# Two DMA queues for x, a new split of the first norm's squares, and fewer idle matmuls at the start

## The chip, the cores and the metric

The kernel runs on one core of a Trainium2 chip. The core has TensorE (PE in the profile) for matrix products, VectorE (DVE) and GpSimd (POOL) for elementwise work, ScalarE (ACT) for functions, and SyncE (SP), which here only issues DMAs. The engines run side by side, each through its own instructions in order, and wait for each other by semaphores. What counts is the device time in microseconds (us). The kernel before took 880.53 us as the median of three runs (880.15 to 881.44).

## What is computed

A two-layer decoder trunk over 1024 positions of width 1024, in float32. Each layer normalises x, scales and shifts it by vectors made from a condition c, mixes it, and adds the gated result to x:

```python
c_act = jax.nn.silu(c)
for layer in range(DEPTH):
    mod = c_act @ ada_w[layer] + ada_b[layer]
    shift, scale, gate = jnp.split(mod, 3, axis=-1)
    h = rmsnorm(x, norm_g[layer]) * (1.0 + scale[:, None, :]) + shift[:, None, :]
    ...  # layer 0: one projection, sliding-window and forgetting attention; layer 1: a recurrent block
    x = x + gate[:, None, :] * y
return rmsnorm(x, final_g)
```

The rmsnorm needs, for each position, the sum of the squares of its 1024 values before anything else can be computed from x. The change concerns that first sum and what stands before it.

## The kernel before

x comes transposed: 128 partitions hold the features, in KT = 8 tiles of 128 features each, and the positions lie along the free axis, in two halves of 512. `xh[0]` and `xh[1]` are the two halves, each of 8 tiles of 128x512 (256 KB each). `col` (128x144) holds every vector that is needed by feature: c, the norm weights, the biases.

The start does this, in this order of program text. GpSimd writes the identity and a tile of ones. SP issues the DMA of `col` (line 149). From c in `col`, ScalarE and VectorE make `cact` = silu(c) (lines 174 to 179); two dummy activations on `tiny2` (lines 180 and 181) have ScalarE load the table that holds Sqrt. From line 415 on, all engines keep the order of the text (`ordered |= ALL`): `load_x(0)` issues the first half of x on SP in five pieces of 2, 2, 2, 1 and 1 tiles; `load_block(c)` issues blocks of ada0 (two rows of 512 KB for the scale and shift of feature tile c, line 395) and of the gate weights (`raws`, `raw_raws`, line 360 on). GpSimd spreads `cact` into `vb8`, and TensorE transposes that into `crow_ps` (line 430), which VectorE then multiplies with ada0's rows (`mod_first`, line 219: one long VectorE instruction for each row).

`warm(n)` (line 423) lets TensorE multiply ones by ones n times; nothing reads the result. In the profile each such matmul, and each transpose or product of float32, stands as two matmul rows. There are `warm(EARLY)` with 12 at the very start, and `warm(WARM)` with 6 at three places: after the transposes of c, after the sums of squares, and after the spread of the norm's factor.

`squares(0)` (line 398) fills eight tiles with squares, `sq[0]` to `sq[7]`, and adds them in pairs: ScalarE squares tiles 0, 2, 4, 6 and 7, VectorE tiles 1, 3 and 5; GpSimd adds 0 and 1, VectorE adds 2 and 3, 4 and 5, 6 and 7. In the profile sq[4], sq[5] are `sq_pth` and sq[6], sq[7] are `sq_ptl`. `norm_sums` then adds over the features on TensorE: each of the four sums gives four matmuls with a two-column right side (eight rows), into `psq_n`. `rstd_of` (line 255) makes the norm's factor from that on VectorE and ScalarE, ending in a copy to `vb_n`; its `spread` has TensorE transpose `vb_n` into `rs_n`. `modulate_in(0, 0, prs)` (line 283) applies factor, scale and shift to tile 0 of x on VectorE (`x`) and ScalarE (`hh`).

Then comes the loop over c = 0 to 7 (line 453): in each step TensorE runs 15 matmuls of 512 columns (`pst`, lines 479 to 483) on tile c of the first half, while the other engines modulate tile c + 1, split its weights into two parts, and load block c + 4. At c = 3 the loop issues further gate weights and `load_x(1)`.

Of the kernel before, what the change touches and what calls it, by code (L numbers as in the profile page):

```python
# [12 lines left out]
F32 = mybir.dt.float32  # L13
F32R = mybir.dt.float32r
AF = mybir.ActivationFunctionType
# [1 line left out]
PSUM = bass.MemoryType.PSUM  # L17

WARM = 6
EARLY = 12  # L20
NS = 5
FIRST = 18
AHEAD = 4
# [1 line left out]
P = 128  # L25
S = 1024
D = 1024
KT = D // P
HALF = 512
# [19 lines left out]
def hybrid_trunk(  # L49
# [23 lines left out]
    ordered = set()  # L73
# [25 lines left out]
    act, dve, gp = Queue("act", nc.scalar), Queue("dve", nc.vector), Queue("gp", nc.gpsimd)  # L99
    pe, sync = Queue("pe", nc.tensor), Queue("sync", nc.sync)  # L100
    ALL = {"act", "dve", "gp", "pe", "sync"}

    def copy(out, in_, scale=1.0):
        act.activation(out, in_, AF.Copy, scale=scale)

    def mul(eng, out, a, b):
        eng.tensor_tensor(out=out, in0=a, in1=b, op=ALU.mult)

    def add(eng, out, a, b):
        eng.tensor_tensor(out=out, in0=a, in1=b, op=ALU.add)  # L110
# [34 lines left out]
    tiny = const.tile([P, 1], F32, name="tiny")  # L145
    gp.memset(tiny, 1e-30)
    tiny2 = const.tile([P, 1], F32, name="tiny2")
    col = const.tile([P, NCOL], F32, name="col")
    sync.dma_start(col, cols)
    nsink = const.tile([P, 8], F32, name="nsink")  # L150
    bfb = const.tile([P, 8], F32, name="bfb")

# [18 lines left out]
        sub(dve, out, l, c)  # L171


    cact = const.tile([P, KT], F32, name="cact")
    ce = const.tile([P, KT], F32, name="ce")
    act.activation(ce, col[:, C_C : C_C + 8], AF.Exp, scale=-1.0)
    dve.tensor_scalar(out=ce, in0=ce, scalar1=1.0, scalar2=None, op0=ALU.add)
    dve.reciprocal(ce, ce)
    mul(dve, cact, ce, col[:, C_C : C_C + 8])
    act.activation(tiny2, cact[:, 0:1], AF.Exp)  # L180
    act.activation(tiny2, tiny2, AF.Sqrt)


    l0 = ctx.enter_context(ExitStack())
    gyp = l0.enter_context(tc.tile_pool(name="gyp", bufs=2, reuse_waits="tile"))
    l0a = ctx.enter_context(ExitStack())
    at = l0a.enter_context(tc.tile_pool(name="at", bufs=2, reuse_waits="tile"))

# [3 lines left out]
    def t4(tag, name, dt=F32, bufs=None):  # L192
        bufs = bufs or BUFS[tag]
        return at.tile([P, 1024], dt, tag=tag, name=name, bufs=bufs)

    xh = []
    for h in range(2):
        t = gyp.tile([P, KT, HALF], F32, tag="gy", name=f"x_{h}")
        xh.append(t)

    mm = pe.matmul

    def tp(out, in_):
        pe.transpose(out, in_, ident)
# [14 lines left out]
    def mod_first(c, part):  # L219

        j = 8 * part + c
        mod_dot(parts[c][part], crow_ps, 0, j, col[:, C_AB0 + j : C_AB0 + j + 1])
        if part:
            g = col[:, C_G0 + c : C_G0 + c + 1]
            act.activation(gsc[:, 0, c : c + 1], mod[:, 0, j : j + 1], AF.Identity, bias=g, scale=g)
# [9 lines left out]
    def norm_sums(sq, w, name, ps=None):  # L235

        psq, steps = sum_steps(sq, w, name, ps)
        for f in steps:
            f()
        return psq  # L240

    def sum_steps(sq, w, name, ps=None):

        psq = (ps or ps_t)(f"psq_{name}")
        sq = sq if isinstance(sq, list) else [sq]

        def step(n, i):
            mm(
                psq[:, 2 * i : 2 * i + 2], sq[n][:, i * P : (i + 1) * P], ones[:, 0:2],
                start=(n == 0 and i == 0), stop=(n + 1 == len(sq) and i + 1 == w // P),  # L250
            )

        return psq, [lambda n=n, i=i: step(n, i) for n in range(len(sq)) for i in range(w // P)]
# [29 lines left out]
    def modulate_in(h, k, prs):  # L283

        x, b = xh[h][:, k], mod[:, 0, k : k + 1]
        dve.scalar_tensor_tensor(out=x, in0=prs, scalar=gsc[:, 0, k : k + 1], in1=x, op0=ALU.mult, op1=ALU.mult)
        act.activation(hh[h][:, k], x, AF.Identity, bias=b)
        act.activation(x, x, AF.Identity, bias=b)
        sub(gp, hlo[h][:, k], x, r32(hh[h][:, k]))
# [28 lines left out]
    def half_of(raw):  # L318
        hi, lo = split_raw(raw[0], [P, 4, P], raw[1])
        return [(hi[:, k], lo[:, k]) for k in range(4)]  # L320
# [20 lines left out]
    gy = [None, None]  # L341
# [25 lines left out]
    def split_start(k):  # L367
        split(raws[k], *(t[:, k % 2] for t in four[k // 2]))
        if k % 4 == 0:
            split(rawb[k], *(t[:, k : k + 4] for t in one))  # L370

    def start_w(i, k):
        return tuple(t[:, k % 2, i] for t in four[k // 2]) if i < 4 else tuple(t[:, k] for t in one)

    def load_x(h):
        for k0, k1 in ((0, 2), (2, 4), (4, 6), (6, 7), (7, 8)):
            sync.dma_start(xh[h][:, k0:k1], xT[:, h, k0:k1])

    hl_ada = {}

    parts = {}
# [1 line left out]
    def load_block(c):  # L383

        if c < 4:
            if c % 2 == 0:
                hl_ada[c // 2] = hl.tile([P, 2, 2, S], F32, tag=f"hl{2 + c // 2}", name=f"ada0_{c}")
            parts[c] = [hl_ada[c // 2][:, c % 2, i] for i in range(2)]
        elif c == 6:
            t = at.tile([P, 2, S], F32, tag="V", name=f"ada0_{c}")  # L390
            parts[c] = [t[:, i] for i in range(2)]
        else:
            parts[c] = [t4("KL" if c == 7 else "P", f"ada0_{c}_{i}") for i in range(2)]
        for i in (1, 0):
            sync.dma_start(parts[c][i], ada0[:, c, i])
        load_start(c)

    def squares(h):

        x = xh[h]  # L400
        t = at.tile([P, 4, HALF], F32, tag="V", name=f"sq_{h}")
        sq = [t[:, i] for i in range(4)]
        sq += [at.tile([P, HALF], F32, tag=t, name=f"sq_{t}_{h}_{i}") for t in ("pth", "ptl") for i in range(2)]
        for k in (0, 2, 4, 6, 7):
            act.activation(sq[k], x[:, k], AF.Square)
        for k in (1, 3):
            mul(dve, sq[k], x[:, k], x[:, k])
        add(dve if h else gp, sq[0], sq[0], sq[1])
        add(dve, sq[2], sq[2], sq[3])
        mul(dve, sq[5], x[:, 5], x[:, 5])  # L410
        for k in (4, 6):
            add(dve, sq[k], sq[k], sq[k + 1])
        return sq[0:KT:2]

    ordered |= ALL
    load_x(0)
    for c in range(4):
        load_block(c)
    vb8 = at.tile([P, KT, P], F32, tag="P", name="vb8", bufs=NP)
# [3 lines left out]
    def warm(n):  # L423
        for _ in range(n):
            mm(pw[:, :P], ones, ones, start=True, stop=True)

    warm(EARLY)
    crow_ps = psX[0].tile([P, S], F32, name="crow_ps")
    for k in range(KT):
        tp(crow_ps[:, k * P : (k + 1) * P], vb8[:, k])  # L430
    warm(WARM)
    sq = squares(0)
    psq = norm_sums(sq, HALF, "n0_0", ps_s)
    mod_first(0, 1)
    warm(WARM)
    spread = rstd_of(psq, HALF, at, ("ptl", "pth"), "n0_0", ps_s)
# [7 lines left out]
    def gate_w(i):  # L444
        return wt[T_GATE + i]

    def gate_raw(i):
        t = t4("P", f"raw_gate_{i}").rearrange("p (k e) -> p k e", k=KT)
        sync.dma_start(t, gate_w(i))
        return [(t[:, 4 * n : 4 * n + 4], f"gate_{i}_{n}") for n in range(2)]  # L450

    ws, graw = [[]], {}
    for c in range(KT):
        if c + 1 < KT:
            split_start(c + 1)
            for i in (1, 0):
                mod_first(c + 1, i)
            modulate_in(0, c + 1, prs)
        if c + 4 < KT:
            load_block(c + 4)  # L460
        if c == 3:
            graw[NS] = []
            for n in range(2):
                t = wp.tile([P, 4, P], F32, tag="wlo", name=f"raw_gate_{n}", bufs=4)
                sync.dma_start(t, gate_w(NS)[:, 4 * n : 4 * n + 4])
                graw[NS].append((t, f"gate_{NS}_{n}"))
            load_x(1)
            for i in range(NS + 1, KT):
                graw[i] = gate_raw(i)
        if c in (5, 6):  # L470
            ws[0] += half_of(graw[NS][c - 5])
        if c == 6:
            for i in range(2):
                copy(crow[:, i * HALF : (i + 1) * HALF], crow_ps[:, i * HALF : (i + 1) * HALF])
            sq = squares(1)
            add(dve, sq[2], sq[2], sq[3])
            add(dve, sq[0], sq[0], sq[1])

        for i in range(NS):
            for n, w in enumerate(start_w(i, c)):  # L480
                mm(sps[i], w, hh[0][:, c], start=(c == 0 and n == 0), stop=False)
        for i in range(NS):
            mm(sps[i], start_w(i, c)[0], hlo[0][:, c], start=False, stop=(c + 1 == KT))
# [23 lines left out]
    psq, steps = sum_steps([sq[2], sq[0]], HALF, "n0_1")  # L507
# [111 lines left out]
    for tb in range(NB):  # L619
        h, o = tb // 4, (tb % 4) * P  # L620
# [54 lines left out]
    for i in range(2):  # L675
        t = t4("P", f"bias_{i}").rearrange("p (h j) -> p h j", h=4)
# [322 lines left out]
    def q_job(ti, name):  # L999
        q = lazy(lambda: qtiles(name))  # L1000
        return q, job(ti, name, lambda h, ps: use_q(q(), name)(h, ps))
# [14 lines left out]
    for p in range(4):  # L1016
        q, jq = q_job(T_AQ + p, f"aq_{p}")
# [19 lines left out]
    k = 0  # L1037
    while ti_ < len(units) or any(x >= k for x in due):
        slot = list(due.pop(k, []))
        if ti_ < len(units) and ti_ in sdone and k > sdone[ti_] + GAP_T:  # L1040
# [3 lines left out]
            t, v = t_left.pop(0)  # L1044
# [541 lines left out]
    for t0, tw in ((0, 512), (512, 256), (768, 256)):  # L1586
        h, o = t0 // HALF, t0 % HALF
# [112 lines left out]
```

## Time and profile before

| | us |
|---|---|
| median of the three runs (lowest, highest) | 880.53 (880.15, 881.44) |
| the profiled execution, its own time | 880.89 |
| its span in the profile | 878.8 |
| TensorE busy in the span | 857.0 (98%) |
| VectorE, ScalarE, GpSimd busy | 566.1, 536.0, 388.9 |

The span is what the profile covers of the execution; 2.1 us of its own time lie outside. Times in the rows below are microseconds from the span's start. A row of the timeline has the start, how long it lasted, the engine, the source line (85 is the line of a helper through which almost everything is issued), the operation, what it writes and reads, the shape, and the count; in square brackets stands how long the engine sat idle before and what ended that. A row of the chain of waits has a start, a duration and the work that held the end up there. In a table of stretches each engine has its busy time and, in brackets, its instructions; then come the clock granted to TensorE (1.00 is 2.4 GHz, 0.50 is 1.2 GHz), the busy share of the DMA engines, and GB/s.

### The profile page before, as it was taken

The numbers are of one execution on the slowest core, as the hardware profiler recorded it, in microseconds if no ns is written. First come the engines' busy times: TensorE is split into PE (matmuls) and PEld (weight loads), VectorE is DVE, ScalarE is ACT, GpSimd is POOL, SyncE is SP. The second block draws the span as 40 slices with busy tenths as digits, with TensorE's granted clock in tenths as the row PEclk, the third lists the DMA queues.
The fourth block names the chain that finished last, engine by engine and source line by source line (L and its number), as shares of the span: only waits on it lengthen the run. The fifth ranks groups of instructions, "written<-read, shape, count | busy, mean of one in ns | idle before, by whom it ended". The sixth has DMA issues, their size and how long they took to land.

```text
span 878.8 us, 13498 instructions
## 1 busy us (share of the span) xinstructions
PE 857.0 (98%) x4618; PEld 728.5 (83%) x4618; DVE 566.1 (64%) x1134; ACT 536.0 (61%) x1047; POOL 388.9 (44%) x429
## 2 busy tenths in 40 slices
PE   9999999999989999999999999999999999989995
PEld 8887898888878888888878888878888877868995
DVE  6886557688676566566656668365677655873543
ACT  5756124788676565666766657356767766874532
POOL 3843232343352232232574555632765566884100
PEclk8999999999999999999999999999999999999998
DMA  9943772100113224322373564421221212326042
GB/s 342 403 174 129 219 235 71 41 25 25 37 43 114 87 81 130 115 92 83 112 231 115 159 211 150 139 74 56 79 77 53 75 43 67 97 83 216 15 146 80
DMA packets 54620, 103.83 MB, mean 118 GB/s; under 512 B 6960, under 2 KB 20720, under 8 KB 54040
## 3 DMA queue, kind: packets, MB, share of 16 engines
q1 hardware_dynamic: 53400, 101.93, 35.0%
q10 hardware_dynamic: 1152, 1.05, 0.4%
q8 instruction: 36, 0.59, 0.3%
q14 instruction: 32, 0.26, 0.1%
HBM read 94.02 MB, written 8.93 MB: 117 GB/s over the span
## 4 chain that ended last, share of the span: by engine, by line
PE 84%; POOL 5%; issue 3%; DVE 2%; ACT 2%; DMA 2%; SPq 0%; POOLq 0%; DVEq 0%; ACTq 0%
PE ps_fill L85 22%; PE pst L85 10%; PE ps_o L85 10%; PE ps_lg L85 7%; PE ps_lx L85 6%; PE ps_o0c L85 5%; PE oB L85 4%; PE sB L85 4%; PE ptB L85 4%; PE ps_v L85 3%; PE sA L85 2%; PE oA L85 1%; PE ptA L85 1%; POOL wlo_lg L85 1%; PE psr L85 1%
## 5 line engine op out<-in xcount | busy, mean ns | idle before, releaser
L85 PE MATMUL ps_o<-y1h,wo 128*128 128x256 f32 (+1 forms) x336 | 76.4, 322 | 0.0
L85 DVE TENSOR_TENSOR ptl_B<-ptB,pth_B 128x512 fp32r<-128x512 f32 (+1 forms) x80 | 50.9, 636 | 35.6 <-ACT pth_B L85 34.9
L85 ACT ACTIVATE pB<-pB,mnB 128x128 f32<-128x128 f32 (+3 forms) x64 | 49.6, 775 | 32.5 <-DVE mnB L85 26.9
L85 ACT ACTIVATE pth_B<-ptB 128x512 fp32r<-128x512 f32 (+1 forms) x80 | 44.2, 552 | 41.1 <-PE ptB L85 40.2
L85 DVE SCALAR_TENSOR_TENSOR xc_r<-ps_lx,col,xc_r 128x509 f32<-128x509 f32 (+2 forms) x48 | 35.7, 745 | 43.4 <-ACT xt_r L85 42.3
L85 PEld LDWEIGHTS ps_o<-y1h,wo 128*128 128x128 f32 x336 | 56.7, 193 | 4.7
L85 POOL TENSOR_SCALAR_AFFINE_SELECT pB<-pB 128x128 f32<-128x128 f32 x64 | 18.8, 295 | 93.5 <-DMA pB<-gd 74.8
L85 PE MATMUL pst<-hh,ws 128*128 128x512 f32 x192 | 55.3, 396 | 0.0
L85 PE MATMUL ps_o<-y1l,wo 128*128 128x256 f32 (+1 forms) x168 | 54.2, 323 | 0.0
L85 PE MATMUL ps_lg<-h1h,wlo_lg 128*128 128x512 f32 x128 | 50.2, 392 | 0.9 <-POOL wlo_lg L85 0.8
L85 PE MATMUL ps_lx<-h1l,whi_lx 128*128 128x512 f32 x128 | 50.3, 393 | 0.2 <-POOL h1l L85 0.2
L85 PE MATMUL ps_lx<-h1h,wlo_lx 128*128 128x512 f32 x128 | 50.4, 393 | 0.1
L85 PE MATMUL ps_lx<-h1h,whi_lx 128*128 128x512 f32 x128 | 50.3, 393 | 0.0
L85 PE MATMUL ps_lg<-h1l,whi_lg 128*128 128x512 f32 x128 | 49.8, 389 | 0.0
L85 PE MATMUL ps_lg<-h1h,whi_lg 128*128 128x512 f32 x128 | 49.8, 389 | 0.0
L85 POOL TENSOR_TENSOR wlo_lx<-raw_lx,whi_lx 128x512 fp32r<-128x512 f32 x16 | 30.6, 1930 | 43.3 <-ACT whi_lx L85 26.8
L85 ACT ACT_TABLE_LOAD x35 | 44.9, 1283 | 5.1 <-issue 3.0
L85 DVE CUSTOM_DVE_ANT_0 pB<-sB,pB 128x384 f32<-128x384 f32 (+2 forms) x64 | 35.3, 555 | 17.9 <-PE sB L85 9.7
L85 PE MATMUL ptB<-ident,pB 128*128 128x128 f32 x288 | 45.2, 274 | 1.4 <-DVE ptl_B L85 0.7
L85 PEld LDWEIGHTS ptB<-ident,pB 128*128 128x128 f32 x288 | 35.7, 140 | 12.7 <-PE rbT_B L85 1.5
L85 PEld LDWEIGHTS pst<-hh,ws 128*128 128x128 f32 x192 | 35.9, 188 | 8.7 <-issue 0.6
L85 DVE CUSTOM_DVE_ANT_0 ada<-ada,crow,col 128x1024 f32<-128x1024 f32 x24 | 31.6, 1342 | 8.8 <-DMA ada<-in_ada_dram 8.8
(312 smaller groups left out, 2837.2 us busy)
## 6 DMA issues: line engine op xcount, KB each, us to landing
ada<-in_ada_dram SPq DMA_DIRECT2D x32, 512.0 KB
x<-in_xT_dram SPq DMA_DIRECT2D x20, 256.0 KB
ada<-in_ada_dram SPq DMA_DIRECT2D x4, 1024.0 KB
pB<-gd SPq DMA_DIRECT2D x8, 512.0 KB
raw_o0a<-in_wo_dram SPq DMA_DIRECT2D x16, 256.0 KB
raw_o0c<-in_wo_dram SPq DMA_DIRECT2D x16, 256.0 KB
x1d<-x SPq DMA_DIRECT2D x16, 256.0 KB
raw_lx<-in_wl_dram SPq DMA_DIRECT2D x16, 256.0 KB
```

Of the source, the lines that this page charges most:

```text
L85: ins = issue(*args, **kw)
```

## The change

`col` is now issued by ScalarE, ahead of everything else on it. The first half of x is issued right after, by two engines: SP issues tiles 0-1, 2-3 and 6, ScalarE tiles 4-5 and 7. These DMAs keep their order on ScalarE and SP. The dummy activation that waited for `cact` is gone; the one on Sqrt reads `tiny` instead. For the first half, ScalarE squares tiles 0, 2, 4, 5, 6 and 7, VectorE tiles 1 and 3, and VectorE makes all four additions; GpSimd has none, and each addition of 0-1 and 2-3 stands right behind the square it needs. `warm(EARLY)` has 9 instead of 12 matmuls; the 6 after the transposes of c are gone, and 2 come after the first four steps of the sum. The second half of x is loaded and squared as before.

```diff
-EARLY = 12
+EARLY = 9
...
-    sync.dma_start(col, cols)
...
+    l0 = ctx.enter_context(ExitStack())
+    gyp = l0.enter_context(tc.tile_pool(name="gyp", bufs=2, reuse_waits="tile"))
+    xh = [gyp.tile([P, KT, HALF], F32, tag="gy", name=f"x_{h}") for h in range(2)]
+
+    def load_x(h, queues):
+        for q, (k0, k1) in zip(queues, ((0, 2), (2, 4), (4, 6), (6, 7), (7, 8))):
+            q.dma_start(xh[h][:, k0:k1], xT[:, h, k0:k1])
+
+    ordered |= {"act", "sync"}
+    act.dma_start(col, cols)
+    load_x(0, (sync, sync, act, sync, act))
...
-    act.activation(tiny2, cact[:, 0:1], AF.Exp)
-    act.activation(tiny2, tiny2, AF.Sqrt)
+    act.activation(tiny2, tiny, AF.Sqrt)
+    ordered.clear()
...
-        for k in (0, 2, 4, 6, 7):
-            act.activation(sq[k], x[:, k], AF.Square)
-        for k in (1, 3):
-            mul(dve, sq[k], x[:, k], x[:, k])
-        add(dve if h else gp, sq[0], sq[0], sq[1])
-        add(dve, sq[2], sq[2], sq[3])
-        mul(dve, sq[5], x[:, 5], x[:, 5])
+        if h == 0:
+            for k in (0, 2, 4, 5, 6, 7):
+                act.activation(sq[k], x[:, k], AF.Square)
+            for k in (1, 3):
+                mul(dve, sq[k], x[:, k], x[:, k])
+                add(dve, sq[k - 1], sq[k - 1], sq[k])
+        else:
+            ...
         for k in (4, 6):
             add(dve, sq[k], sq[k], sq[k + 1])
...
     ordered |= ALL
-    load_x(0)
...
-    warm(WARM)
     sq = squares(0)
-    psq = norm_sums(sq, HALF, "n0_0", ps_s)
+    psq, steps = sum_steps(sq, HALF, "n0_0", ps_s)
+    for i, f in enumerate(steps):
+        f()
+        if i == 3:
+            warm(2)
     mod_first(0, 1)
     warm(WARM)
...
-            load_x(1)
+            load_x(1, [sync] * 5)
```

## Rows read from the trace of the kernel before

**Rows 1.** The page: busy time, share of the span, instructions of each engine.
```profile
PE 857.0 (98%) x4618; PEld 728.5 (83%) x4618; DVE 566.1 (64%) x1134; ACT 536.0 (61%) x1047; POOL 388.9 (44%) x429
```
**Rows 2.** The chain of waits in the first 60 us, in order of time.
```profile
1.66 4.82 DMA x<-in_xT_dram
...
12.64 2.77 PE warm L85 x12
15.41 0.85 PE rs_n L85 x4
16.26 2.32 PE warm L85 x12
18.58 35.64 PE pst L85 x154
```
**Rows 3.** Timeline of VectorE in the first 20 us.
```profile
5.23 0.69 DVE L85 TENSOR_TENSOR sq<-x 128x512 f32<-128x512 f32 x1 [1.70 <-DMA x<-in_xT_dram]
6.50 1.39 DVE L85 TENSOR_TENSOR sq<-x 128x512 f32<-128x512 f32 x1 [0.58 <-DMA x<-in_xT_dram]
...
10.01 0.69 DVE L85 TENSOR_TENSOR sq_ptl<-sq_ptl,sq_ptl 128x512 f32<-128x512 f32 x1
...
12.68 0.17 DVE L85 TENSOR_SCALAR psq_n<-psq_n 128x8 f32<-128x8 f32 x1 [0.79 <-PE psq_n L85]
...
13.96 0.69 DVE L85 COPY vb_n<-psq_n 128x512 f32<-128x512 f32 x1
```
**Rows 4.** Timeline of ScalarE in the first 20 us.
```profile
0.73 1.28 ACT L85 ACT_TABLE_LOAD   x1 [0.73 <-PEq L1689]
2.67 0.21 ACT L85 ACTIVATE ce<-col 128x8 f32<-128x8 f32 x1 [0.66 <-DMA col<-in_cols_dram]
...
7.80 0.63 ACT L85 ACTIVATE sq_pth<-x 128x512 f32<-128x512 f32 x1 [0.67 <-DMA x<-in_xT_dram]
8.47 1.29 ACT L85 ACTIVATE sq_ptl<-x 128x512 f32<-128x512 f32 x2
...
17.09 0.72 ACT L85 ACTIVATE hh<-x,mod 128x512 fp32r<-128x512 f32 x1 [2.99 <-DVE x L85]
```
**Rows 5.** Timeline of GpSimd in the first 20 us.
```profile
6.08 1.27 POOL L85 TENSOR_TENSOR sq<-sq 128x512 f32<-128x512 f32 x1 [1.45 <-DVE sq L85]
```
**Rows 6.** Timeline of TensorE in the first 20 us.
```profile
5.52 1.04 PE L85 MATMUL crow_ps<-ident,vb 128*128 128x128 f32 x8
...
10.15 1.05 PE L85 MATMUL psq_n<-ones,sq_pth 128*128 128x2 f32 x8 [0.34 <-DVE sq_pth L85]
11.06 1.58 PE L85 MATMUL psq_n<-ones,sq_ptl 128*128 128x2 f32 x8
```
**Rows 7.** Timeline of SP's DMA issues in the first 20 us.
```profile
0.74 0.40 SPq L85 DMA_DIRECT2D col<-in_cols_dram  x1
1.20 2.54 SPq L85 DMA_DIRECT2D x<-in_xT_dram  x5
```
**Rows 8.** Table of short stretches, TensorE alone: busy, granted clock, DMA share, GB/s.
```profile
11.30:11.40 0.10, 0.10 (x3) 0.80 1.35 369
...
18.10:18.20 0.10, 0.10 (x3) 0.57 0.99 410
```
**Rows 9.** Timeline of ScalarE's DMA issues at 130 us.
```profile
129.91 0.35 ACTq L679 DMA_DIRECT2D bias<-rd  x1
```
**Rows 10.** DMA queues from 131 to 131.5 us: packets, MB, share of engines.
```profile
q10 hardware_dynamic: 31, 0.03, 28.2%
q1 hardware_dynamic: 20, 0.05, 24.8%
```
**Rows 11.** Timeline near the end of the first loop, from 38 to 46 us.
```profile
38.72 0.63 ACT L85 ACTIVATE whi_gate<-raw_gate 128x512 fp32r<-128x512 f32 x1 [0.79 <-DMA raw_gate<-in_wt_dram]
...
40.97 0.72 ACT L85 ACTIVATE hh<-x,mod 128x512 fp32r<-128x512 f32 x1 [0.82 <-DVE x L85]
...
42.84 2.50 PE L85 MATMUL pst<-hh,ws 128*128 128x512 f32 x10
```

More of the change, by code (lines that the diff above doesn't have):

```diff
@@ L179, in hybrid_trunk @@
     mul(dve, cact, ce, col[:, C_C : C_C + 8])
-    act.activation(tiny2, cact[:, 0:1], AF.Exp)
-    act.activation(tiny2, tiny2, AF.Sqrt)
-    l0 = ctx.enter_context(ExitStack())
-    gyp = l0.enter_context(tc.tile_pool(name="gyp", bufs=2, reuse_waits="tile"))
+    act.activation(tiny2, tiny, AF.Sqrt)
+    ordered.clear()
     l0a = ctx.enter_context(ExitStack())
@@ L194, in t4 @@
         return at.tile([P, 1024], dt, tag=tag, name=name, bufs=bufs)
[L196 to L199, printed above, removed]
     mm = pe.matmul
@@ L373, in start_w @@
         return tuple(t[:, k % 2, i] for t in four[k // 2]) if i < 4 else tuple(t[:, k] for t in one)
-    def load_x(h):
-        for k0, k1 in ((0, 2), (2, 4), (4, 6), (6, 7), (7, 8)):
-            sync.dma_start(xh[h][:, k0:k1], xT[:, h, k0:k1])
     hl_ada = {}
@@ L403, in squares @@
         sq += [at.tile([P, HALF], F32, tag=t, name=f"sq_{t}_{h}_{i}") for t in ("pth", "ptl") for i in range(2)]
-        for k in (0, 2, 4, 6, 7):
-            act.activation(sq[k], x[:, k], AF.Square)
-        for k in (1, 3):
-            mul(dve, sq[k], x[:, k], x[:, k])
-        add(dve if h else gp, sq[0], sq[0], sq[1])
-        add(dve, sq[2], sq[2], sq[3])
-        mul(dve, sq[5], x[:, 5], x[:, 5])
+        if h == 0:
[5 more added lines that the diff above has]
+        else:
+            for k in (0, 2, 4, 6, 7):
+                act.activation(sq[k], x[:, k], AF.Square)
+            for k in (1, 3):
+                mul(dve, sq[k], x[:, k], x[:, k])
+            add(dve, sq[0], sq[0], sq[1])
+            add(dve, sq[2], sq[2], sq[3])
+            mul(dve, sq[5], x[:, 5], x[:, 5])
         for k in (4, 6):
```

## The prediction

> **What bounds the kernel now.** I read the page first: TensorE is busy for 857.0 us of the span [rows 1]. So time is won only where TensorE has no useful work or runs slowly. Next, the chain of waits over the first 60 us, to see where that is [rows 2]. From 18.58 on it is one run of `pst` matmuls without a gap: the first loop is bound by TensorE, and whatever the start gains or loses reaches the end only by moving that first `pst`. Before it the chain goes through the landing of x, the squares, the sums on TensorE, then 12 idle rows (12.64 to 15.41), the four transposes of `rs_n`, 12 more idle rows (16.26 to 18.58), and `pst`. So the question is the start of `pst`, with everything after it moving along.
>
> Third, the timelines of the engines, for why the squares end when they do. VectorE's first square starts as x lands (5.23), the next at 6.50, and ScalarE's on tile 4 at 7.80 [rows 3, 4]: a piece of 512 KB each 1.27 to 1.30 us. The second of the two squares that begin at 8.47 starts at 8.47 + 1.29 - 0.63 = 9.13, when the last tile has come [rows 4]. The last addition runs from 10.01 to 10.70 [rows 3]. The sums that need it run on TensorE from 11.06 to 12.64, and VectorE takes them at 12.68 [rows 3, 6].
>
> Fourth, the clock. It is granted in full until 11.36 (the stretch 11.30 to 11.40 shows 0.80 on the way from 1.00 to 0.50, that is from 2.4 to 1.2 GHz) and again from 18.18 (0.57 in 18.10 to 18.20) [rows 8]. It fell while TensorE was on the two-column sums, and rose after idle matmuls and transposes had run without a pause. Eight rows of the sums took 1.05 us at the high level, and 1.58 mostly at the low one [rows 6]. The low level also holds the chain: `vb_n` is there at 13.96 + 0.69 = 14.65, but the idle rows last until 15.41; `hh` is there at 17.09 + 0.72 = 17.81, but the idle rows last until 18.58 [rows 2 to 4].
>
> **The change part by part.** *The start of the transfers.* x's first piece was issued at 1.20, behind `col`, which took SP from 0.74 [rows 7]. It moves to 0.74: 0.46 us sooner for the whole of x, if the same bytes flow at the same rate. The last tile then lands at 9.13 - 0.46 = 8.67.
>
> The Trainium skill (DMA: Bandwidth & Descriptors, "Issuing engines are not separate DMA queues") says that issuing from several engines saves only the issuing time, since all DMAs share the same 16 engines. By that, the second queue itself gives nothing, and the sum keeps just these 0.46 us; no row of x here can show it, since SP alone issues x.
>
> *The order of landing* is not in this trace, so it is bounded. One end: the pieces land in the old order, each 0.46 sooner. ScalarE then starts on tile 4 at 7.80 - 0.46 = 7.34, squares 4, 5, 6, 7 back to back (4 x 0.63), ends at 9.86, and the last addition ends 0.69 later, at 10.55: 0.15 sooner than 10.70. The other end: the two queues share evenly. Tiles 4-5 then take half the rate from tiles 0-1 and 2-3. The first piece would land at 4.77 alone; the second queue starts some 0.46 behind it (one issue of 0.40 lies ahead of it), so the remaining 0.8 us take 1.6, and it lands near 5.6; tiles 4-5 land at 6.5, tile 7 at 7.8, tiles 2-3 only near 7.95. ScalarE takes tile 2 ahead of 4, 5, 6, 7, so five squares follow 7.95: 7.95 + 5 x 0.63 = 11.1, and with the addition 11.8: 1.1 later. The nearest row is at 130 us: ScalarE issued a DMA at 129.91, and in the half microsecond from 131 its queue (q10) and SP's (q1) both had packets moving, for 28.2% and 24.8% of the engines' time [rows 9, 10]. So the queues do share. I take a value between the ends, since `col` lies ahead of tiles 4-5 in their queue.
>
> *The squares.* VectorE's square of tile 3 took 1.39 us, against 0.69 for tile 1, and GpSimd's addition (6.08 to 7.35) lay over it [rows 3, 5]. With that gone, the square should take 0.69: 0.7 us of VectorE. VectorE also loses the square of tile 5 (0.69) and gains an addition of 0.69. All that comes free ahead of the last addition, which waits for ScalarE's last square: ScalarE gains one square, 0.63, counted above. What VectorE wins shows in TensorE: before, the last group of sums began at 11.06, 0.36 after its addition, since the group ahead was late. Counting these 0.36 as won at the lower end, and lost again if the sums run at the low clock, the end of the sums shifts by -0.5 to +1.1.
>
> *ScalarE's issues.* Three issues of about 0.40 stand ahead of the first table load (1.28): `ce` starts at 0.74 + 3 x 0.42 + 1.28 = 3.3 instead of 2.67 [rows 4, 7]. If the load is first, ScalarE's DMAs are later by 1.28 instead, which lies inside the two ends above. `cact`, `vb8` and the transposes of c come some 0.65 later: from 5.52 to 6.56 before, so to about 6.5 or 7.2 now [rows 6]. They stand ahead of the sums on TensorE, whose first group needs tile 0's sum, at about 6.4 to 7.1. Hidden; without that cover it would be 0.65 of the first group, and it is still four groups to the end. Moving `col` past SP's x costs the second engine nothing else: GpSimd's and VectorE's first work on `col` is the same `cact` chain.
>
> *Idle matmuls.* Three at the start and six after the transposes go; two are added amid the sums. Those removed stood before x's sums existed, so they held nothing back: zero. Two cost at most 4 rows of 0.2, ahead of sums that are not there yet. What they may cost or give is the clock, below.
>
> *The sum.* At the low clock the work between the end of the sums and `pst` is 12.64 to 18.58, nearly all TensorE's; the rise at 18.18 cuts it. If rise and fall stay where they are, a shift of the sums by s changes how much idle work is left at 18.18, and that runs twice as fast after it: `pst` moves by s/2, so by -0.25 to +0.55. The middle is +0.15, which is nothing beside the other terms. Against the profiled 880.89 (span 878.8 and 2.1 outside) that is no change; the median, 880.53, is 0.36 below that execution. I forecast 880.5.
>
> **The rivals.** *The clock is kept or comes back sooner.* If the sums end earlier, the following idle matmuls start earlier, and the clock might rise before `pst` by some microseconds or never fall. Without the low clock, from the end of the sums: 1.97 to `vb_n` (12.68 to 14.65), half of 0.85 for `rs_n`, and 1.55 from there (16.26) to the end of `hh` (17.81): 4.0 instead of 5.94, so 1.95 sooner. But not all of that gets through: at 38.72 ScalarE waits for a transfer of gate weights, the chain from there ends with `hh` of the last tile at 41.69, and TensorE wants that at 42.84 [rows 11]. The slack is 1.15, plus 0.46 if the transfers are all sooner: 1.6 at most. So 878.9. For it: the idle rows now gate the chain. Against: the two-column sums remain, and with fewer idle matmuls about them.
>
> *The clock stays low into the loop: slower.* The low stretch lasted 6.8 us here [rows 8]. The change leaves TensorE with less work between 5 and 8 us, and the clock may fall sooner; sums at 1.58 for eight rows are then the bound (three groups, 4.7 us from tile 2's sum), the idle matmuls begin later, and the rise may come after `pst` has started. If the low level lasts twice as long from 11.36, to 25.0, `pst` runs from about 18.6 at half rate for 6.4 us: 3.2 us lost, 883.7. It decides over "no change" from 1.76 us, that is when the rise comes after 22.1. Against it: the idle matmuls in front of `pst`, which raised the clock before, are all still there.
>
> *A transfer hidden anyway*: if the pieces come in the old order and the first sums are not late, the 0.46 us are spent on ScalarE's sixth square (0.63), and nothing is left. That is the lower end above, and the same 880.5 within 0.3.
>
> **How the numbers follow.** The measurement of this kernel tells about 0.2% from no change, 1.76 us: 878.8 to 882.3. Forecast with both ends of landing: 0.60, all of it inside. The clock kept: 0.25, mostly inside since its gain is capped at 1.6, about half of it beyond if the cap is lower than thought. Low into the loop: 0.13, nearly all slower. Something downstream, where the order of instructions is planned anew: 0.02. Faster 0.14, same 0.73, slower 0.13. The range of 878.6 to 882.2 takes in the forecast, the kept clock and the mild end of the late one.
>
> **What would show it.** x's first issue at about 0.74, the last square of ScalarE ending between 9.9 and 11.1, tile 2's square before or after 7 us (old order or even shares); VectorE's square of tile 3 at 0.69; the last sum on TensorE between 12.1 and 13.7; the clock low from 11.4 at the latest until 18.2; the first `pst` between 18.3 and 19.1; `hh` of the last tile still ahead of its matmuls. I am wrong if the clock's rise moves, or if the first `pst` moves and the end of the span doesn't.

## The result, and the profile after

The changed kernel takes 885.14 us in the median of 18 runs (880.94 to 886.26), the kernel before 880.39 beside it: a ratio of 1.0050 (95% interval 1.0039 to 1.0060). It is slower by 4.75 us, and lies 2.9 us above the predicted range. The profiled execution took 885.6 us, with a span of 883.8 against 878.8.

The page, first busy times of the engines, as in [rows 1]. TensorE has 14 matmul rows fewer (4604 against 4618) and is busy 1.7 us longer:

```profile
PE 858.7 (97%) x4604; PEld 729.7 (83%) x4604; DVE 564.1 (64%) x1134; ACT 535.8 (61%) x1047; POOL 389.2 (44%) x428
```

The chain of waits of the changed kernel, its first pieces, against [rows 2]. It no longer begins with x but with `col`, and goes through the transposes of c and all the sums:

```profile
0.73 4.25 DMA col<-in_cols_dram
...
7.41 1.97 PE crow_ps L85 x8
...
11.94 4.91 PE psq_n L85 x24
16.85 2.77 PE warm L85 x12
...
21.81 35.88 PE pst L85 x154
```

The timeline of TensorE in the first 22 us, against [rows 6]:

```profile
1.13 4.21 PE L85 MATMUL warm<-ones 128*128 128x128 f32 x18 [1.13 <-POOL tiny L85]
7.41 1.97 PE L85 MATMUL crow_ps<-ident,vb 128*128 128x128 f32 x8 [2.07 <-POOL vb L85]
9.17 1.71 PE L85 MATMUL psq_n<-ones,sq 128*128 128x2 f32 x8
10.74 1.20 PE L85 MATMUL warm<-ones 128*128 128x128 f32 x4
11.73 1.71 PE L85 MATMUL psq_n<-ones,sq 128*128 128x2 f32 x8
13.30 1.84 PE L85 MATMUL psq_n<-ones,sq_pth 128*128 128x2 f32 x8
15.01 1.84 PE L85 MATMUL psq_n<-ones,sq_ptl 128*128 128x2 f32 x8
16.71 2.91 PE L85 MATMUL warm<-ones 128*128 128x128 f32 x12
19.41 0.80 PE L85 MATMUL rs_n<-ident,vb_n 128*128 128x128 f32 x4
20.04 1.50 PE L85 MATMUL warm<-ones 128*128 128x128 f32 x12
21.81 0.50 PE L85 MATMUL pst<-hh,ws 128*128 128x512 f32 x1 [0.26 <-ACT hh L85]
```

The transposes start at 7.41 instead of 5.52, behind 2.07 us in which TensorE stands still for `vb`, and take 1.97 instead of 1.04. Eight rows of the sums take 1.71 to 1.84 instead of 1.05 (1.58 for the last eight). These are the durations of the low clock; 12 idle rows take 2.91 at 16.71 and 1.50 at 20.04, so it rises just before 20. It had not been up before: no rows ahead of that run at the faster pace. (The column of the granted clock prints 1.00 from 0 to 19.8: it prints that until the trace has its first change, whatever the rows show. The same holds for the kernel before until about 4.5.)

VectorE and ScalarE in the same stretch, against [rows 3, 4]:

```profile
5.77 0.68 DVE L85 TENSOR_TENSOR sq<-x 128x512 f32<-128x512 f32 x1
...
7.89 0.69 DVE L85 TENSOR_TENSOR sq<-x 128x512 f32<-128x512 f32 x1
...
9.89 0.69 DVE L85 TENSOR_TENSOR sq_ptl<-sq_ptl,sq_ptl 128x512 f32<-128x512 f32 x1
...
16.89 0.17 DVE L85 TENSOR_SCALAR psq_n<-psq_n 128x8 f32<-128x8 f32 x1 [5.11 <-PE psq_n L85]
```
```profile
2.15 1.28 ACT L85 ACT_TABLE_LOAD   x1 [2.15 <-issue]
5.00 0.21 ACT L85 ACTIVATE ce<-col 128x8 f32<-128x8 f32 x1 [1.57 <-DMA col<-in_cols_dram]
...
8.71 1.13 ACT L85 ACTIVATE sq_ptl<-x 128x512 f32<-128x512 f32 x2
```

The squares do what they should: tile 3 takes 0.69, the last addition ends at 10.58 (10.70 before). But the sums that need it are there only at 16.85, and VectorE stands 5.11 us for them. And `ce`, the first step that needs `col`, starts at 5.00 instead of 2.67.

Why `col` comes late is seen in the queues. The table of DMA queues of the changed kernel from 2.5 to 3.5 us (packets, MB, share of the engines); q1 is SP's, with x, q10 ScalarE's, with `col`:

```profile
q1 hardware_dynamic: 62, 0.25, 75.0%
q10 hardware_dynamic: 52, 0.03, 13.3%
```

The queues take turns, about a packet each, but a packet of x is 4 KB (0.25 MB in 62) and one of `col` 0.6 KB. So `col`, 72 KB, goes at the pace of x beside it. Before, it went ahead of x in one queue. The Trainium skill (DMA: Bandwidth & Descriptors, "Queues, rings and completion order") says that each DMA engine goes round-robin between the queues that have work, a packet at a time. The trace agrees as to equal turns, 62 against 52; the page's packet can hold several descriptors, and no run shows whether the profile counts the same thing.

Not all of the 5.0 us lies at the start. `pst` starts at 21.81 instead of 18.34, 3.5 later. The last large product, `ps_o`, by its groups (count, min/median/max in ns, first and last start), in the changed kernel:

```profile
L85 PE MATMUL ps_o<-y1h,whi_wo x24: 278/283/504, 775.2 to 851.7; 128*128 128x256 f32 x16, 128*128 128x512 f32 x8
...
L85 PE MATMUL ps_o<-y1l,wo x168: 278/283/628, 785.3 to 872.7; 128*128 128x256 f32 x112, 128*128 128x512 f32 x56
```

and in the kernel before:

```profile
L85 PE MATMUL ps_o<-y1h,whi_wo x24: 278/283/504, 771.5 to 846.7; 128*128 128x256 f32 x16, 128*128 128x512 f32 x8
...
L85 PE MATMUL ps_o<-y1l,wo x168: 280/283/628, 780.4 to 867.7; 128*128 128x256 f32 x112, 128*128 128x512 f32 x56
```

Its first matmul starts 3.7 us later and its last 5.0: 1.3 us are lost inside it. The waits of TensorE show where, first the changed kernel, then the one before:

```profile
PE ps_o L85 <- ACT y1h L85: 2.8, 1, 2.8
```
```profile
PE ps_o L85 <- ACT y1h L85: 1.6, 1, 1.6
```

and the waits of ScalarE from 764 to 780 us in the changed kernel name a block of wo's weights that lands late; `y1h` comes behind the step that waits for it, on the same engine:

```profile
ACT wo L85 <- DMA raw_wo<-in_wo_dram: 1.4, 1, 1.4
```

The order of the instructions there is the same in both kernels. What makes that block late is the subject of the last experiment.

### The profile page after: what moved, and what is told of

The parts are those of the page before. It is cut to its first block, busy times and chain, and to the rows that moved or that the text cites. A ratio compares the mean times of both kernels' runs of the same rounds, so it can differ in the third digit from the quotient of the medians.

```text
span 883.8 us, 13467 instructions
## 1 busy us (share of the span) xinstructions
PE 858.7 (97%) x4604; PEld 729.7 (83%) x4604; DVE 564.1 (64%) x1134; ACT 535.8 (61%) x1047; POOL 389.2 (44%) x428
## 4 chain that ended last, share of the span: by engine, by line
PE 77%; POOL 7%; issue 5%; ACT 4%; DVE 4%; DMA 3%; SPq 0%; POOLq 0%; DVEq 0%; ACTq 0%
PE ps_fill L85 22%; PE ps_o L85 10%; PE ps_lx L85 6%; PE ps_lg L85 6%; PE ps_o0c L85 5%; PE pst L85 5%; PE oB L85 4%; PE sB L85 4%; PE ptB L85 3%; PE ps_v L85 2%; PE sA L85 2%; PE oA L85 1%; POOL wlo_lg L85 1%; PE ptA L85 1%; DMA raw_wv<-in_wv_dram 1%
## 5 line engine op out<-in xcount | busy, mean ns | idle before, releaser
L85 ACT ACTIVATE sq_o<-x 128x512 f32<-128x512 f32 (+1 forms) x33 | 18.0, 546 | 30.5 <-DVE x L85 30.2
```

What stands on the lines that cost most here:

```text
L85: ins = issue(*args, **kw)
```

## The experiments

The change has three parts: the transfers (T), the squares (S) and the idle matmuls (I: 9 instead of 12 at the start, six behind the transposes of c taken away, two put amid the sums). The results up to here allowed two causes: `col` comes late, or the clock comes late for want of idle matmuls. The first five runs take the parts singly and in pairs.

**S and I, without T.** The changed kernel with the transfers of before:

```diff
+    sync.dma_start(col, cols)
...
-    act.dma_start(col, cols)
-    load_x(0, (sync, sync, act, sync, act))
...
-    act.activation(tiny2, tiny, AF.Sqrt)
-    ordered.clear()
+    act.activation(tiny2, cact[:, 0:1], AF.Exp)
+    act.activation(tiny2, tiny2, AF.Sqrt)
...
+    load_x(0)
...
```

> The changed kernel with its transfers as before: SP issues col and then all of x, and the dummy activations are the old ones; squares and idle matmuls stay as changed. Theory 1, the column vectors come too late (4.98 us in the changed kernel): here col lands near 2.6, the transposes of c run by 5.5, the sums of squares end by 13, the first loop starts by 18.6, and the time is 879.5 to 881. Theory 2, the missing idle matmuls keep the clock low: the granted clock still rises only at 18 to 20 us, the sums take 0.2 us a row, the first loop starts at 20 or later, and the time is 882.5 to 885.

Measured: 882.01 us, ratio 1.0019 (1.0010 to 1.0028).

**T and S, without I.**

```diff
-EARLY = 9
+EARLY = 12
...
+    warm(WARM)
     sq = squares(0)
...
-        if i == 3:
-            warm(2)
...
```

> The changed kernel with the idle matmuls as before (12 at the start, 6 after the transposes of c, none amid the sums); transfers and squares stay as changed. Theory 1 (late column vectors): the transposes still wait for GpSimd's copy until about 7.4, the first loop starts at 20 to 22, time 883 to 886. Theory 2 (clock): the clock is up before the sums of squares, they end by 14, time 880 to 881.5.

Measured: 879.50 us, ratio 0.9997 (0.9988 to 1.0006). `ce` is as late as in the changed kernel (4.97), and it costs nothing: the late `col` alone is not the cause.

**S alone.** The kernel before with

```diff
-        for k in (0, 2, 4, 6, 7):
...
-        add(dve if h else gp, sq[0], sq[0], sq[1])
...
+        if h == 0:
+            for k in (0, 2, 4, 5, 6, 7):
...
+                add(dve, sq[k - 1], sq[k - 1], sq[k])
...
```

> The kernel before with the new split of the squares alone. Both theories: col lands and the clock rises as before. VectorE's square of tile 3 takes 0.69 instead of 1.39, the last addition ends within 0.3 us of 10.7, and the time is that of before within 0.6 us (879.8 to 881).

Measured: 879.04 us, ratio 0.9990 (0.9981 to 0.9998). The split of the squares is a gain of 0.1%, and the only version of this study whose interval lies below 1. First `pst` at 17.41. With the new transfers the split goes the same way (T and S 879.50, T alone 880.52 below).

**T alone.** The changed kernel with the squares and the idle matmuls of before.

```diff
-EARLY = 9
+EARLY = 12
...
-        if h == 0:
-            for k in (0, 2, 4, 5, 6, 7):
...
+        add(dve if h else gp, sq[0], sq[0], sq[1])
...
+    warm(WARM)
     sq = squares(0)
...
```

> The kernel before with the new transfers alone (col and two pieces of x on ScalarE's queue, the dummy activation on tiny). Theory 1: col lands at about 5, the transposes start at about 7.4 and hold the sums behind them, the first loop starts 1.5 us or more later than at 18.6, time 882.5 to 885. Theory 2: the idle matmuls bridge the wait, the clock is up, time 880 to 881.5.

Measured: 880.52 us, ratio 1.0010 (0.9998 to 1.0022).

**I alone.** The kernel before with

```diff
-EARLY = 12
+EARLY = 9
...
-    warm(WARM)
     sq = squares(0)
...
+        if i == 3:
+            warm(2)
```

> The kernel before with the fewer idle matmuls alone (9 at the start, none after the transposes of c, 2 amid the sums). Theory A (what counts is whether TensorE's clock rises before the sums of squares, and 9 idle matmuls are often too short a stretch for that): the time is 1 to 3 us above before, 881 to 883.5, with col landing as early as before. Theory B (late column vectors alone): the time of before, 879.5 to 880.8.

Measured: 882.68 us, ratio 1.0036 (1.0021 to 1.0050). So the idle matmuls hold the loss, about 3 us by themselves (this run against the kernel before, and 882.01 against 879.04), and T adds to it only together with I: 885.14 against 882.01, but 879.50 against 879.04. In the profile of I alone (883.7) the clock does fall, at 8.3, behind 1.37 us in which TensorE waits for x's first sum, and stays low until 18.6. At this point I took all of it for the clock. That was only half right.

**How `col` is issued.** Two runs ask whether it was late for its queue or for its neighbour. In the first, x goes through SP alone and `col` has ScalarE's queue to itself (9 idle matmuls, as changed); in the second, `col` is first on SP, and ScalarE issues its pieces of x beside it (S in, idle matmuls of before).

```diff
-    load_x(0, (sync, sync, act, sync, act))
+    load_x(0, [sync] * 5)
```

> The changed kernel, but SP issues all five pieces of x; only col is on ScalarE. If col is late because its small packets share the engines with x, it still lands near 5 us and the time stays that of the changed kernel, 883.5 to 886. If it is late because two pieces of x lie on ScalarE's own queue, col lands near 3 us, the transposes of c follow the idle matmuls without a gap, and the time is 881 to 882.5.

```diff
-    act.dma_start(col, cols)
+    sync.dma_start(col, cols)
     load_x(0, (sync, sync, act, sync, act))
```

> The new squares and the new queues for x, idle matmuls as before, and col first on SP instead of ScalarE. Sharing theory: the first piece on ScalarE's queue now starts beside col, so col is still late, at 3.5 to 5 us, and the time is within 0.6 us of the run with the idle matmuls undone (879.5). Queue theory (col is late for its queue): col lands near 2.6, the transposes run by 5.5, and the time is 0.5 us or more below the run with the squares alone, 878 to 878.6.

Measured: 885.21 us, ratio 1.0057 (1.0036 to 1.0078), with `ce` at 4.21, between the 3 and the 5 us of the two readings; and 880.22 us, ratio 1.0005 (0.9995 to 1.0014), with `ce` at 5.08. Packets of the second from 2.5 to 3.5 us, where q10 now carries x and q1 `col`:

```profile
q10 hardware_dynamic: 58, 0.24, 79.3%
q1 hardware_dynamic: 51, 0.03, 12.2%
```

`col` is late beside any queue with x in it, wherever it is issued. (Alone in its queue it came 0.8 us sooner than in the changed kernel; what x behind it in its own queue adds is not shown.) Single executions of the first run differ much (880.3 to 886.5). Its profile is of the fastest one: there the sums ran at the high clock, and `pst` began at 16.73.

**Three idle matmuls more.** The changed kernel with only

```diff
-EARLY = 9
+EARLY = 12
```

> The changed kernel with 12 instead of 9 idle matmuls at the start; the 6 after the transposes of c stay out. Theory A (the length of the first idle stretch decides whether the clock rises): nearly all of the loss comes back, 879.5 to 882, with the sums at 0.13 us a row in the profile. Theory A' (the 6 idle matmuls after the transposes matter as much): 882.5 to 885. Theory B (late col): 884 to 886.

Measured: 879.80 us, ratio 1.0006 (0.9991 to 1.0021): six matmul rows give back the whole loss in ten of twelve executions; the other two took 883.6 and 883.9. TensorE's timeline in this run, with the sums at the high clock:

```profile
1.13 5.49 PE L85 MATMUL warm<-ones 128*128 128x128 f32 x24 [1.13 <-POOL tiny L85]
7.56 1.09 PE L85 MATMUL crow_ps<-ident,vb 128*128 128x128 f32 x8 [0.95 <-POOL vb L85]
8.49 0.95 PE L85 MATMUL psq_n<-ones,sq 128*128 128x2 f32 x8
...
11.54 1.03 PE L85 MATMUL psq_n<-ones,sq_ptl 128*128 128x2 f32 x8
...
17.25 2.59 PE L85 MATMUL pst<-hh,ws 128*128 128x512 f32 x10 [0.62 <-ACT hh L85]
```

**Nine, and the six put back.** The changed kernel with

```diff
+    warm(WARM)
     sq = squares(0)
```

> The changed kernel with the six idle matmuls after the transposes of c back, still 9 at the very start. Two readings of why the clock misses its rise are open. (A) It is the length of the first uninterrupted run of TensorE that counts, the one before the transposes (1.13 to 5.34 with 9 idle matmuls): then putting six back behind the transposes changes little before the sums, the clock is low in the sums in most executions, and the time stays near the changed kernel's, 883 to 886 us. (B) It is how much TensorE does in all before the sums: then six more matmuls (12 rows of about 0.2 us, 2.5 us, from 9.4) do as much as three at the start, and the time is 879 to 881, as with 12 at the start.

Measured: 883.35 us, ratio 1.0041 (1.0022 to 1.0061), in the range of (A). The median stands between two groups: four executions of 880.9 to 882.3, with a granted clock of 0.992 to 0.994 over the whole (that figure, too, counts the time ahead of the first change as full speed), and four of 884.4 to 886.0, with 0.987 or 0.988. The profiled one (884.4) is of the second. TensorE's timeline, and a table of stretches (TensorE's busy time, granted clock, DMA share, GB/s):

```profile
1.13 3.90 PE L85 MATMUL warm<-ones 128*128 128x128 f32 x18 [1.13 <-POOL tiny L85]
7.32 1.40 PE L85 MATMUL crow_ps<-ident,vb 128*128 128x128 f32 x8 [2.29 <-POOL vb L85]
8.51 2.77 PE L85 MATMUL warm<-ones 128*128 128x128 f32 x12
11.07 1.10 PE L85 MATMUL psq_n<-ones,sq 128*128 128x2 f32 x8
...
19.05 2.74 PE L85 MATMUL warm<-ones 128*128 128x128 f32 x12
21.47 0.78 PE L85 MATMUL pst<-hh,ws 128*128 128x512 f32 x2
```
```profile
7.90:8.10 0.20, 0.20 (x4) 0.70 0.97 379
8.50:10.50 2.00, 2.00 (x12) 0.50 1.01 402
...
14.70:14.90 0.20, 0.20 (x4) 0.76 0.89 348
21.50:21.70 0.20, 0.20 (x3) 0.67 0.97 369
```

Here the clock had come up (18 idle rows in 3.90 us, 4.21 in the changed kernel), and fell at 8 us, behind the 2.29 us in which TensorE had nothing. It was back at 11.4, so the sums themselves ran at the high clock for the most part, which (A) did not expect. The time went beside them: 12 idle rows at the low clock hold the sums back to 11.07, and from 14.8 to 21.6 the clock is low again, up to `pst`, which starts 3.1 us later than in the kernel before. So the pause that the late `col` leaves after 9 idle matmuls works both ways: the clock doesn't rise, or falls again before the sums.

**More of them.** Three attempts at a better version: the changed kernel with 18 idle matmuls at the start, S alone with two idle matmuls after each of the first three groups of sums, and x on SP alone with 12 at the start.

```diff
-EARLY = 9
+EARLY = 18
```

> The changed kernel with 18 instead of 9 idle matmuls at the very start, enough to keep TensorE busy until the vectors of c have come: 36 rows at 0.21 us until the clock rises and 0.1 after it, so they end near 7 us, against transposes that can start at 7.4. The theory of the clock says that the rise comes before 7 us in every execution, the sums run at 0.13 us a row, the first pst starts between 17 and 18.5, the time is 878.5 to 880, and the spread between executions is smaller than that of the changed kernel. The rival, that the late vectors themselves cost the time, says 883 or more.

```diff
+        if i in (3, 7, 11):
+            warm(2)
```

> The kernel before with the new split of the squares, and two idle matmuls after each of the first three groups of sums; transfers and the other idle matmuls as before. If the sums' two-column matmuls are what lets the clock fall at 11 to 13 us, idle matmuls between them may hold it: then no fall before the loop, the first pst near 16.5 to 17, and 878 to 878.8, a little under the split of the squares alone (879.0). If the fall comes anyway, the added rows only cost (12 rows of 0.1 to 0.2 us, some of it hidden): 879 to 880.5.

```diff
-EARLY = 9
+EARLY = 12
...
-    load_x(0, (sync, sync, act, sync, act))
+    load_x(0, [sync] * 5)
```

> The changed kernel with all of x on SyncE's queue, the vectors alone on ScalarE's, and 12 idle matmuls at the start. With 9 idle matmuls the same transfers took 885.2 in the median and 880.3 in the one execution in which the clock had risen before the sums. Theory of the clock: the three matmuls bring the median down to 878.5 to 880. Rival, that these transfers are bad of themselves: it stays above 882.

Measured: 880.21 us, ratio 1.0007 (0.9994 to 1.0019); 880.11 us, 1.0003 (0.9992 to 1.0015); 879.23 us, 1.0007 (0.9992 to 1.0023). None beats the kernel before. With eighteen the executions lie no closer together (877.5 to 882.7) than with twelve (878.1 to 883.9), so that part of the expectation was wrong. In the second, the sums do stay at the high clock (0.95 each), but the added rows lie on the path, the clock falls behind the sums all the same (12 idle rows take 2.91 from 13.69), and `pst` starts at 18.94. The third confirms that those transfers are not bad of themselves. It also shows that twelve are not always enough beside a late `col`: five of its executions took 881.2 to 884.2, and in the profiled one of them (881.8) the clock fell at 9.2, stayed low until 19.5, and `pst` started at 20.59.

**Nine alone, and the six alone.** On the kernel before, where `col` is early:

```diff
-EARLY = 12
+EARLY = 9
```

> The kernel before with 9 instead of 12 idle matmuls at the very start and nothing else changed. If the first run of TensorE is what decides (theory A of the run with six put back, which came out at 883.4), the clock misses its rise before the sums in a good part of the executions and the median is 881.5 to 883.5. If only the idle matmuls in all count, or TensorE's pause before the transposes has to come on top, the six after the transposes, which stand here, make up for it, and the time is 880 to 881.

```diff
-    warm(WARM)
     sq = squares(0)
...
+        if i == 3:
+            warm(2)
```

> The kernel before with the six idle matmuls after the transposes taken away and two put amid the sums, 12 at the very start as before. If the first run decides, this costs nothing: 879.5 to 880.8. If the six count as much as the three at the start, the sums run at the low clock and the time is 881.5 to 883.

Measured: 880.02 us, ratio 1.0005 (0.9993 to 1.0016), and 879.63 us, 0.9999 (0.9988 to 1.0011). Neither costs anything; for the first that is against theory A, which had 881.5 to 883.5. All combinations now (medians in us, not all taken at the same time; "six" are those behind the transposes; starred ones with the new squares):

| idle matmuls | rows fewer | `col` early | `col` late |
|---|---|---|---|
| 12, six | 0 | 880.4, 879.0* | 880.5, 879.5*, 880.2* |
| 12, none | 8 | 879.6 | 879.8*, 879.2* |
| 9, six | 6, with `col` late 2 | 880.0 | 883.4* |
| 9, none | 14 | 882.7, 882.0* | 885.1*, 885.2* |

The last column says that 9 at the start are too few once `col` is late, six or none behind. The last line says something else: with `col` early, either group may go, but not both. And in the profile of S and I without T the clock is no later than before (18 idle rows in 3.77 us, `pst` at 18.05), yet the kernel is 3 us slower than S alone in the median. What all four kernels of the last line share is the longer wait for `y1h`: 2.6 to 2.8 us in their profiles, 1.5 or 1.6 in the other twelve. It goes with the number of matmul rows. Instructions come through queues of their own; for one of them the page of the changed kernel (packets, MB, share) has

```profile
q8 instruction: 36, 0.59, 0.3%
```

that is 16 KB each, and 0.59 MB over 2 x 4604 matmuls and weight loads is 64 bytes each, so by its size it is TensorE's. With 14 rows fewer at the start, each later fetch would come 14 matmuls later against the work. In the kernel before, a fetch stands at 766.5 to 767 us, over 2 us ahead of the issue of that block of wo (769.1); in the changed kernel at 773.5 to 774, behind the issue (772.8).

**Fourteen rows, taken elsewhere.** The kernel before with 12 at the start and the clock up in time:

```diff
-    warm(WARM)
     sq = squares(0)
...
     prs = spread()
-    warm(WARM)
+    warm(WARM - 1)
```

> The kernel before with the six idle matmuls after the transposes taken away and five instead of six behind the spread of the factor: 14 matmul rows fewer, with all 12 idle matmuls at the start and none amid the sums. Theory of the fetch: each row fewer lets TensorE's instructions be fetched one matmul (about 0.23 us) later against the work, so 14 rows move the fetch by some 3.2 us, from about 2.5 us ahead of the issue of that block of wo (769.1 in the kernel before) to some 0.7 us behind it; TensorE waits 2.6 to 2.8 us there, and the time is about 1.1 us more than with 8 rows fewer (which was 0.3 above the kernel before): some 1 to 1.5 us above the kernel before of the same call. Rival, that the wait belongs to the 9 idle matmuls at the start or to the low clock: it stays 1.5 to 1.6 us, and the time is within 0.5 us of the kernel before. In either case the clock is up before the sums, and the first pst starts near 17 to 18.5.

Measured: 882.10 us, ratio 1.0027 (1.0018 to 1.0037). The sums run at the high clock, `pst` begins at 17.05, earlier than in the kernel before, and the wait is there. TensorE's wait, ScalarE's timeline at 770 us, and the instruction queue in the half microsecond from 769.0, with 14 rows fewer:

```profile
PE ps_o L85 <- ACT y1h L85: 2.7, 1, 2.7
```
```profile
770.46 0.65 ACT L85 ACTIVATE wo<-raw_wo 128x512 fp32r<-128x512 f32 x1
772.39 0.63 ACT L85 ACTIVATE wo<-raw_wo 128x512 fp32r<-128x512 f32 x1 [1.29 <-DMA raw_wo<-in_wo_dram]
```
```profile
q8 instruction: 1, 0.02, 18.5%
```

The wait and the timeline in the run of the six alone, with eight rows fewer, which issues its blocks of wo at the same moment (768.3); its fetch stands 1.5 us earlier, in the half microsecond from 767.5 (last row):

```profile
PE ps_o L85 <- ACT y1h L85: 1.5, 1, 1.5
```
```profile
770.44 1.37 ACT L85 ACTIVATE wo<-raw_wo 128x512 fp32r<-128x512 f32 x2
```
```profile
q8 instruction: 1, 0.02, 16.9%
```

Six rows move the fetch by 1.5 us, about 0.25 a row, from 0.5 us ahead of a block's issue to 1.0 behind it, and ScalarE waits 1.29 us for the second of its two pieces. That the number of matmul rows does it, and not the clock at the start, is shown.

What the fetch does to the block can be read from the completions that the trace keeps, sixteen for each block. With 14 rows fewer, fifteen of those of the first block come from 770.40 to 770.87 and the last at 772.37, and ScalarE goes on at 772.39; with eight fewer all sixteen come from 770.33 to 771.15. In all five kernels with the wait, the fetch begins 1.0 to 1.1 us behind the issue and lasts 1.3 to 1.6 us, and the last completion comes 0.9 to 1.5 us behind the fifteenth. In the twelve others the fetch begins at least 0.5 us ahead of the issue, and that gap is 0.1 to 0.4 us. So one sixteenth of the first block is what comes late. That it shares a DMA engine with the fetch fits (the one packet took 18.5% of sixteen engines' half microsecond, 1.48 us of one engine), but the records don't name the engine.

The price was mis-sized: expected 1 to 1.5 us above the kernel before, measured 2.5. The wait explains 1.2. The rest goes with the clock: the ten executions were granted 0.988 to 0.992 over the whole, the fourteen of the kernel before beside them 0.991 to 0.994, and where both have 0.992 (two and seven executions) they are only 1.3 us apart in the mean. In the profiles the clock was low near 780 us for 6.8 us here, for 3.4 in the kernel before, and not at all in the run with eight rows fewer; `ps_o` lasted 97.8, 96.2 and 94.7 us from its first start to its last. Whether the wait brings the low clock on is not shown: the lengths differ between executions of kernels without the wait, too.

## Why the prediction was wrong

The forecast was no change, 880.5 us; 885.14 came. Two causes together make the 4.75 us, and each has a run of its own: the clock that stays low, or falls again, ahead of `pst` when `col` is late and 9 idle matmuls stand at the start (the run with the six put back, about 3 us, where `pst` started 3.1 later), and the 14 rows fewer, which push a fetch behind the issue of a block of wo (2.5 us, of which 1.2 is the wait itself). Their sum is a little over what was measured, within the intervals.

- *"Those removed stood before x's sums existed, so they held nothing back: zero."* This is the step that failed. As waits they were indeed nothing. But they are what TensorE does while the clock is low, and they are places in its program. The first could have been seen in the timeline of TensorE in the kernel before, where 24 idle rows take 4.56 us, 0.19 each, and the next 12 take 0.125 each, so that the clock rose during the first:

```profile
1.13 4.56 PE L85 MATMUL warm<-ones 128*128 128x128 f32 x24 [1.13 <-POOL tiny L85]
...
6.40 1.50 PE L85 MATMUL warm<-ones 128*128 128x128 f32 x12
```

- *"Granted in full until 11.36."* The column was taken at its word for a stretch in which the trace has no record of the clock. That hid that the start is at the low level, and that the sums' pace depends on the rise coming in time.
- *ScalarE's issues: `ce` at 3.3, transposes at 6.5 to 7.2, hidden.* The step counted only the time to issue. `ce` came at 5.00, the transposes at 7.41. The halving of rates was worked out for the pieces of x, and not for the one small transfer beside them, which suffers most. By itself this was hidden, as the step said (T and S without I: no loss); the cover is gone only with the fewer idle matmuls.
- *The start of the transfers, the order of landing, the squares.* x's first issue came at 0.74 and tile 3's square took 0.69, as forecast. But "0.46 us sooner for the whole of x" did not hold: by the completions in the trace the first piece landed at 4.80 (5.20 before), tiles 2-3 at 7.09 and tiles 4-5 at 7.58, between the two ends, and the last tile at 9.08, against 8.67 in the sum and 9.11 before. That the last addition still ended at 10.58, near the lower bound of 10.55, is luck: ScalarE's six squares began only at 6.63, behind the late `col` and a table load, and ran to 9.84 at about 0.53 us each instead of 0.63. How much the 0.7 us of VectorE give is not shown by itself; S alone gained 0.1%, and in its profile the clock was also low for a shorter time (13.6 to 17.0).
- *`pst` moves by s/2* rested on a rise that stays at 18.18. It came at 19.8 in the changed kernel, and at 17.0 in S alone. It is not a fixed point.
- *"Reaches the end only by moving that first `pst`."* Wrong for 1.3 of the 5.0 us. An edit also reaches the end by moving instruction fetches against transfers elsewhere. In the other direction a gain is capped, as the rival put it: with nine matmuls alone `pst` starts 1.4 us earlier, at 17.0, and its last matmul starts only 0.8 earlier, at 109.2.
- *The rival "the clock stays low into the loop"* had the right cause (less work for TensorE between 5 and 8 us) and sign, with 883.7 us, but another place: it had the low level begin at 11.36 and slow `pst` itself. Instead the clock was not up before 19.8, and the sums, transposes and idle rows took it all; `pst` ran at full speed. The chance of 0.13 was too small, because it was argued that the idle matmuls in front of `pst` would bring the clock back. They did, 1.6 us later than before.

Of what the prediction said would prove it wrong, the first came at once: the rise moved, and the first `pst`, forecast for 18.3 to 19.1, started at 21.8.

## What to carry to other kernels

Matmuls whose result nobody reads are not free to remove: ask what clock the rows behind them run at, from the rows' own durations, and count how many instructions leave the engine's program. A small transfer that the first chain needs should be alone in the queues until it has landed; beside large packets it came 1.5 to 2.5 us later here. When two parts of a change each cost nothing, run them together before calling them harmless.

## What the runs showed of the hardware that was not expected

- A 72 KB transfer of small packets was there at 2.67 us when it went ahead of x in one queue, and at 4.2 to 5.2 us beside a queue with 4 KB packets, whichever of the two queues carried it.
- Fourteen matmul rows (seven idle matmuls) fewer at the start moved a 16 KB instruction fetch that stands some 750 us further on in the program, and the kernel took 2.5 us longer. The Trainium skill (Runtime: NRT & Kernel Launch, "Instruction fetch mechanics") says that instructions are refilled in blocks of 16 KiB, and that "The cost of crossing a 16 KiB boundary is one DMA tail-bump, mostly hidden." The size agrees (36 packets, 0.59 MB). The cost seen here is another one, to the transfer beside the fetch: it was hidden in all twelve kernels in which the fetch stood ahead of the transfer, and not in the five in which it stood behind its issue.
- The moment of the clock's first rise is not the same from kernel to kernel with the same idle rows, nor between executions: 24 idle rows took 4.55 us in T alone and 5.49 in S alone. Single executions of the changed kernel lie between 880.9 and 886.3. Its one profile is of a long execution (885.6); that the short ones meet the clock in time is likely, as the fastest execution of the run with x on SP alone (880.3) did in its profile.
